# Gated MLP in a two-layer trunk: order of the first products of two pairs, place of the sums of squares and of the scales

## The chip, the cores and the metric

The kernel runs on one core of a Trainium2 chip. The metric is the device time of one execution, in microseconds. Of the kernel before, three executions were timed: 2381.71, 2385.93 and 2390.98, median 2385.93. One more execution was profiled.

## What is computed

Two layers of a decoder trunk over 1040 positions (16 meta tokens and 1024 tokens) of 1024 numbers, in float32. Layer 0 mixes by a short convolution and a gated DeltaNet, layer 1 by attention in a sliding window. Behind each mixer stands the same gated MLP with a causal convolution of width 3 on its gate half. The change is in that MLP alone.

```python
D_MODEL = 1024
SEQ = 1024
N_META = 16
D_FF = 2816
...
def rms_norm(x, w):
    xf = x.astype(jnp.float32)
    y = xf * lax.rsqrt(jnp.mean(xf * xf, -1, keepdims=True) + EPS)
    return (y * w.astype(jnp.float32)).astype(x.dtype)
...
def conv_ffn(h, w_up, conv_w, w_down):
    gate, val = jnp.split(h @ w_up, 2, -1)
    gate = causal_dwconv(gate, conv_w)
    return (jax.nn.silu(gate) * val) @ w_down
...
    for layer in range(DEPTH):
        i = layer // 2
        hn = rms_norm(h, attn_norm_w[layer])
        ...
        h = h + mix.astype(h.dtype)
        ff = conv_ffn(rms_norm(h, ffn_norm_w[layer]), ffn_w_up[layer], ffn_conv_w[layer], ffn_w_down[layer])
        h = h + ff.astype(h.dtype)
    return h[:, N_META:]
```

## The kernel before

The activations lie with the 1024 features on partitions, as eight tiles `h[0..7]` of 128 x 1040. All products are made in float32 precision from two parts: an operand is split into a high part (a cast to the matmul format, on ScalarE, called ACT) and a low part (operand minus high part, on VectorE, called DVE), and TensorE (PE) adds up high x high, high x low and low x high.

`ffn` (L706) makes the up projection in 22 pairs (`NF`). Pair i is one block of 128 gate columns (weights `wg`) and one block of 128 value columns (`wv`). The two token halves and the two feature halves make a 2 x 2 block product that is done with seven products instead of eight, in the manner of Strassen and Winograd. Each of the seven has an operand X0 to X6, built once per layer on ACT and DVE out of `h` and the norm's weights (`parts`, L746; four 128 x 520 pieces with high and low part each, X63 being the last piece of X6), and weights that are `wg`, `wv` or sums of their halves: `sa` (L876, L877) and `sb` (L887, L888). The norm's scale per token, `rstd`, is applied only to the result (L904). A product is 24 matmuls: two token quarters, four feature pieces, three part products.

In each pair X0, X2, X4 and X5 go one after the other into the PSUM tile `A`, with copies `p1`, `u2`, `u3` taken in between on ACT (`snap`, L829). X1 goes into a tile `C`, X3 and X6 into another `C`. `A` and `C` have two buffers each. From these copies come `r` (gate) and `v` (value): `r` takes X1's tile (L871) and X6's (L903), is scaled (L904), convolved and passed through tanh (L851 to L860), and multiplied with `v` (L906); `v` takes X3's tile (L894) and X5's (L898). X6 is added into the same PSUM tile that L894 reads, so X6 waits for L894. The product is stored (`fy`) and read again by the down projection, as `yf`, scaled (L927) and split (L928, L929).

Entry of the MLP: the squares of `h` are summed over the eight tiles into a tile `r` (L737 to L741). `scales` (L758) multiplies the sums with ones on PE (L761) into a `C` tile and finds `rstd` from it on ACT and DVE (L765 to L770), for each token half. The source has both scales ahead of pair 0. The residual stream `h` is stored to memory (`hd`, L735) while its operands are built in place.

Who sets the order: the code is written in program order, and a scheduler of the framework lists each engine's instructions from it, moving them ahead or back by its own estimates; each engine then runs its list strictly in order. `issue_after` holds a part back behind a given instruction. All loads and stores are issued on the SP queue. The matmuls of the out projections ahead of the MLP (L147) use a ring of PSUM tiles `mm` that are freed by the adds into `h` (L699 in layer 0, L1188 in layer 1; two buffers in layer 1). Weights are split into `whi` (L814) and `wlo` (L815), in buffers that turn over three places, one in pool `fp` and two in pool `wp`. The down projection's first weights (`wdr`, cast `wdh` L134 on ACT, low part `wdl` L135 on GpSimd, called POOL) use the buffers of `wp` too.

## Time and profile before

| | |
|---|---|
| median of three executions | 2385.93 us (2381.71 to 2390.98) |
| the profiled execution's own time | 2385.68 us |
| its span in the profile | 2383.9 us |
| mean granted TensorE clock | 0.994 |
| PE busy | 2324.3 us (98%) |
| DVE busy | 1615.8 us (68%) |
| ACT busy | 973.4 us (41%) |
| POOL busy | 408.2 us (17%) |

The MLP of layer 0 starts at 583.78 us of the span and its up projection ends near 1041; that of layer 1 starts at 1668.55 and ends near 2134.

How to read the lines in the prediction. A row of the timeline gives start and length in us, engine, source line, operation, output and input by the program's names, and in brackets how long the engine stood idle before it and what released it. A row of the wait table gives engine, waiting group and releaser, then the total, the number of waits and the longest. A row of the windows gives a stretch, its length, the busy time of PE, PEld (weight loads), DVE, ACT and POOL with the number of instructions, the granted clock, the DMA share and GB/s. A row of the chain gives start, length and the group that lies on the chain of work that ended last. Lengths on DVE include a start-up that overlaps the instruction before, so the distance from start to start is the cost of one.

### The profile page before, as it was taken

How to read it: one execution, taken by the hardware profiler on the slowest of the kernel's cores; microseconds unless marked ns; L12 is line 12 of the kernel's file. 1: busy time of each engine (PE TensorE's matmuls, PEld its weight loads, DVE VectorE, ACT ScalarE, POOL GpSimd, SP SyncE). 2: the span in 40 equal slices, each digit the busy share in tenths (PEclk: the TensorE clock that was granted, in tenths of full speed). 3: DMA queues.
4: the chain of work that ended last, by engine and by line, in shares of the span. 5: the costliest groups of instructions: out<-in, count | busy, mean ns of one | idle time of the engine just before them, and what ended most of it. 6: DMA issues, size and time to landing. Idle time of an engine off the chain costs nothing.

```text
span 2383.9 us, 39785 instructions
## 1 busy us (share of the span) xinstructions
PE 2324.3 (98%) x16000; PEld 2182.5 (92%) x16000; DVE 1615.8 (68%) x2799; ACT 973.4 (41%) x1952; POOL 408.2 (17%) x357
## 2 busy tenths in 40 slices
PE   8999999999999999999999999999899999999999
PEld 7989999999999999999999986778799999987887
DVE  8886745566877777777436466768977777778332
ACT  6544313434444444433116456656544444443110
POOL 1123323431000000012225233231000000002221
PEclk9999999999999999999999999999899999999999
DMA  4233534241222222154223110203222222234222
GB/s 139 79 128 121 170 111 138 76 161 72 89 81 81 81 76 76 63 188 139 66 60 129 45 36 19 89 27 116 81 89 81 81 81 77 72 142 169 76 67 102
DMA packets 93481, 224.83 MB, mean 94 GB/s; under 512 B 18672, under 2 KB 30264, under 8 KB 93296
## 3 DMA queue, kind: packets, MB, share of 16 engines
q1 hardware_dynamic: 93296, 222.28, 27.1%
q8 instruction: 126, 2.06, 0.3%
q14 instruction: 59, 0.48, 0.1%
HBM read 166.08 MB, written 56.15 MB: 93 GB/s over the span
## 4 chain that ended last, share of the span: by engine, by line
PE 84%; DVE 10%; ACT 3%; DMA 1%; issue 1%; POOL 0%; SPq 0%; ACTq 0%; DVEq 0%; POOLq 0%
PE mm L147 40%; PE A L825 20%; PE C L825 15%; PE scp L1067 1%; DVE qt L251 1%; PE po L1122 1%; DVE X L752 1%; PE qkp L971 1%; PE po L1125 1%; ACT xh L182 0%; DVE Xd L499 0%; DVE yl L171 0%; DVE fq L497 0%; DMA rb<-rq 0%; PE ptp L1096 0%
## 5 line engine op out<-in xcount | busy, mean ns | idle before, releaser
L825 PE MATMUL A<-X,whi 128*128 128x260 f32 (+1 forms) x2816 | 513.3, 283 | 5.6 <-ACT whi L814 3.2
L147 PE MATMUL mm<-y,wdh 128*128 128x346 f32 (+2 forms) x1760 | 471.0, 350 | 1.6 <-DVE r L903 1.6
L825 PEld LDWEIGHTS A<-X,whi 128*128 128x128 f32 x2816 | 434.0, 189 | 7.2 <-ACT whi L814 3.6
L825 PE MATMUL C<-X,whi 128*128 128x260 f32 (+1 forms) x2112 | 393.7, 285 | 7.8 <-DVE v L894 5.9
L825 PE MATMUL A<-X,wlo 128*128 128x260 f32 (+1 forms) x1408 | 392.6, 283 | 1.3 <-DVE wlo L815 1.3
L147 PEld LDWEIGHTS mm<-y,wdh 128*128 128x128 f32 x1760 | 315.1, 188 | 32.7 <-DVE r L903 2.0
L135 POOL TENSOR_TENSOR wdl<-wdr,wdh 128x512 fp32r<-128x512 f32 (+1 forms) x80 | 118.8, 1485 | 1311.7 <-ACT wdh L134 1302.4
L825 PEld LDWEIGHTS C<-X,whi 128*128 128x128 f32 x2112 | 330.7, 190 | 8.9 <-DVE v L894 6.3
L147 PE MATMUL mm<-y,wdl 128*128 128x346 f32 (+2 forms) x880 | 307.5, 350 | 0.6 <-POOL wdl L135 0.6
L825 PE MATMUL C<-X,wlo 128*128 128x260 f32 (+1 forms) x1056 | 297.5, 284 | 0.0
L825 PEld LDWEIGHTS A<-X,wlo 128*128 128x128 f32 x1408 | 264.2, 189 | 1.5 <-DVE wlo L815 1.5
L939 DVE TENSOR_TENSOR h<-mm,h 128x346 f32<-128x346 f32 (+2 forms) x200 | 115.9, 584 | 201.8 <-PE mm L147 201.0
L825 PEld LDWEIGHTS C<-X,wlo 128*128 128x128 f32 x1056 | 200.4, 190 | 0.0
L147 PEld LDWEIGHTS mm<-y,wdl 128*128 128x128 f32 x880 | 165.5, 188 | 16.8 <-POOL wdl L135 1.3
L815 DVE TENSOR_TENSOR wlo<-sa,whi 128x1024 fp32r<-128x1024 f32 x44 | 53.9, 1226 | 161.8 <-ACT whi L814 161.8
L134 ACT CAST wdh<-wdr 128x512 fp32r<-128x512 f32 (+1 forms) x80 | 53.1, 663 | 255.6 <-PE mm L147 221.9
L814 ACT CAST whi<-sb 128x512 fp32r<-128x512 f32 x88 | 54.7, 621 | 132.7 <-PE C L825 131.0
L147 PE MATMUL mm<-xl,wqkvh 128*128 128x346 f32 (+1 forms) x288 | 95.8, 333 | 1.4 <-DVE xl L183 1.4
L147 PE MATMUL mm<-xh,wqkvh 128*128 128x346 f32 (+1 forms) x288 | 96.3, 337 | 0.7 <-DVE row L269 0.7
L814 ACT CAST whi<-sa 128x1024 fp32r<-128x1024 f32 x44 | 46.1, 1048 | 115.7 <-PE A L825 115.0
L147 PE MATMUL mm<-xh,wqkvl 128*128 128x346 f32 (+1 forms) x288 | 93.0, 325 | 0.0
L928 ACT CAST y<-yf 128x346 fp32r<-128x346 f32 (+2 forms) x110 | 54.7, 536 | 93.1 <-DVE yf L927 73.7
(391 smaller groups left out, 5054.1 us busy)
## 6 DMA issues: line engine op xcount, KB each, us to landing
wg<-in_w_up SPq DMA_DIRECT2D x44, 512.0 KB, 3.2
wv<-in_w_up SPq DMA_DIRECT2D x44, 512.0 KB, 3.3
wdr<-in_w_down SPq DMA_DIRECT2D x48, 256.0 KB, 2.6
fy<-sg SPq DMA_DIRECT2D x22, 520.0 KB, 2.7
yf<-fy SPq DMA_DIRECT2D x22, 520.0 KB, 4.1
fy<-sg SPq DMA_DIRECT2D x22, 516.0 KB, 2.7
yf<-fy SPq DMA_DIRECT2D x22, 516.0 KB, 4.7
wdr<-in_w_down SPq DMA_DIRECT2D x32, 320.0 KB, 3.5
```

Source lines behind the costliest of these rows:

```text
L134: ac.copy(hi, raw)
L135: eng.tensor_tensor(lo, raw, hi.bitcast(F32), ALU.subtract)
L147: pe.matmul(ps[:, :n], a[:, j, :], b[:, c0:c0 + n], start=(i == 0), stop=(i == last))
L251: ve.scalar_tensor_tensor(d, buf[:, pad + c0 - i:pad + c0 - i + n], taps[W - 1 - i], tmp[:, :n], ALU.mult, ALU.add)
L752: last_lo[:] = [ve.tensor_tensor(lo, src, hi.bitcast(F32), ALU.subtract).ins]
L814: ac.copy(hi, src)
L815: ve.tensor_tensor(lo, src, hi.bitcast(F32), ALU.subtract)
L825: pe.matmul(ps[:, b, :q], a[:, at + k, :], x[:, c], start=(start and n == 0), stop=(n == 11), skip_group_check=not start)
L928: ac.copy(yh[:, s], yf[:, s])
L939: ve.tensor_tensor(hn[m][:, s], ps[:, :n], hn[m][:, s], ALU.add)
L971: pe.matmul(p2[:, :n], ct[:, C_BD:C_BD + P], sq, start=True, stop=True)
L1067: pe.matmul(ps[:, :nk], qg[G][t][r, tok], kx[G][r, cols], start=True, stop=True)
```

## The change

Five things. (1) Pair 0's weights are loaded, and their sums `sa0`, `sb0` and the split of `sa0` are written, ahead of everything else in `ffn`. The pools of raw weights are swapped between odd and even pairs, and the three-place rotation of the split weights is shifted. (2) The squares are summed in the two halves of `rstd` instead of an `r` tile. (3) The two `scales` stand behind pair 0's third product (X2) instead of ahead of pair 0; they work in place in `rstd`, with an `sg` and a `th` tile for scratch. (4) The first two products of pair 1 (X0, X1) are written right behind the first two of pair 0. (5) `v` has two buffers instead of one; the four t2 pieces of the operands lie in two `v` tiles, and the separate t2 tiles are gone. The number of products, sums and casts stays the same.

```diff
+                    nw = [0]
+
+                    def wtile():
+                        nw[0] += 1
+                        p = fp if nw[0] == 1 or nw[0] > 2 and nw[0] % 3 == 2 else wp
+                        t = tuple(p.tile([P, KT, P], F32R, tag=tag, name=tag) for tag in ("whi", "wlo"))
+                        return t
...
+                    def weights(i):
+                        raws = []
+                        for n, at in (("wg", i), ("wv", NF + i)):
+                            r = (wp if i % 2 else fp).tile([P, KT, P], F32, tag="wraw", name=n, **({} if i % 2 else {"bufs": 2}))
+                            sp.dma_start(r, w_up[layer, at])
+                            raws.append(r)
+                        return raws
+
+                    def s21(raws):
+
+                        (wg, wv) = raws
+                        sa = fp.tile([P, KT, P], F32, tag="ws", name="sa", bufs=2)
+                        ve.tensor_tensor(sa[:, 4:8], wv[:, 0:4], wv[:, 4:8], ALU.add)
+                        ve.tensor_tensor(sa[:, 0:4], sa[:, 4:8], wg[:, 0:4], ALU.subtract)
+                        return sa
...
+                    raws0 = weights(0)
+                    sa0 = s21(raws0)
+                    w20 = wtile()
+                    wsplit(w20, 0, KT, sa0)
+                    sb0 = s34(raws0, sa0)
+
+
+                    ss = [rstd[:, tk[s]] for s in range(2)]
-                    sums = full("r", 2)
-                    ss = [sums[:, s * hf:s * hf + hf] for s in range(2)]
...
-                        t = full("th")[:, :hf]
-                        ay = full("sg")
+                        ay, t = full("th" if s else "sg"), rstd[:, tk[s]]
...
-                            ve.scalar_tensor_tensor(rstd[:, tk[s]] if i else y, t, m3, y, ALU.add, ALU.mult)
+                            ve.scalar_tensor_tensor(t if i else y, t, m3, y, ALU.add, ALU.mult)
...
-                    vt2 = full("v")
-                    t2 = [half("t2", 2, "t2") if k < 2 else vt2[:, (k - 2) * hf:(k - 1) * hf] for k in range(4)]
+                    vt2 = [full("v", 2) for _ in range(2)]
+                    t2 = [vt2[k // 2][:, k % 2 * hf:(k % 2 + 1) * hf] for k in range(4)]
...
                     half_x = last_lo[0]
-                    for s in range(2):
-                        scales(s)
...
-                        p = fp if nw[0] % 3 == 0 else wp
...
-                            r = (fp if i % 2 else wp).tile([P, KT, P], F32, tag="wraw", name=n, **({"bufs": 2} if i % 2 else {}))
...
-                        raws = weights(i)
+                        raws = weights(i) if i else raws0
...
+                    def second(w1, p1):
+
                         Bk = wide("C")
                         product(Bk, w1, 4, 1, True)
                         r = full("r", 2)
                         ve.memset(r[:, 0:2], 0.0)
                         ve.tensor_tensor(two(r[:, 2:2 + hf]), Bk[:, :, :q], two(p1), ALU.add)
+                        return r
+
+
+                    nxt = first(0)
+                    rs = [second(*nxt[1::2])]
+                    ahead = first(1)
+                    rs.append(second(*ahead[1::2]))
+                    for i in range(NF):
+                        (wg, wv), w1, A, p1 = nxt
+                        v2 = wv[:, 4:8]
+                        r = rs[i] if i < 2 else second(w1, p1)
+                        if i == 0:
+                            sa, w2, sb = sa0, w20, sb0
+                        else:
+                            with tc.issue_after(half_x) if i == 1 else nullcontext():
+                                sa = s21((wg, wv))
+                                w2 = wtile()
+                                wsplit(w2, 0, KT, sa)
                         product(A, w2, 0, 2, False)
                         u2 = snap("u2", A)
+                        if i == 0:
+                            for s in range(2):
+                                scales(s)
...
-                        v = full("v")
+                        v = full("v", 2)
                         ve.tensor_tensor(two(v[:, hf:2 * hf]), two(u3), C[:, :, :q], ALU.subtract)
                         if i + 1 < NF:
-                            nxt = first(i + 1)
+                            nxt = first(i + 1) if i else ahead
```

What that does to the lists of the engines is shown at three places. Line numbers of the changed kernel differ: L852 is the product's matmul (L825 before), L804 the scale's (L761), L741 the weights' low part (L815), L784 the sum of squares (L741), L755 and L756 `sa`, L763 and L764 `sb`, L923 `v` (L894), L879 and L935 the end of the gate (L860, L906), L958 the split of `y` (L929), L798 an X piece (L755), L1217 the add into `h` (L1188).

First, PE at the start of the MLP of layer 0, before. L147 is the end of the out projection, X03 the last piece of X0, X10 the first of X1. This is where the second scale stands:

```order
L825 MATMUL A_6163<-X03_6031,whi_6159 128x260 x2
L825 MATMUL A_6163<-X03_6031,wlo_6160 128x260
L761 MATMUL C_6098<-r_5969,ct_68 128x260 x2
L825 MATMUL C_6190<-X10_6034,whi_6159 128x260 x2
L825 MATMUL C_6190<-X10_6034,wlo_6160 128x260
L825 MATMUL C_6190<-X11_6037,whi_6159 128x260 x2
```

The first scale stands right behind the out projection, the second between X0 and X1 of pair 0. After the change both scales stand here, on the same engine (A_6145 is pair 0's tile):

```order
L852 MATMUL A_6145<-X23_6082,whi_5976 128x260 x2
L852 MATMUL A_6145<-X23_6082,wlo_5977 128x260
L804 MATMUL C_6289<-rstd_69,ct_68 128x260 x2
L852 MATMUL A_6145<-X40_6098,whi_6338 128x260 x2
L852 MATMUL A_6145<-X40_6098,wlo_6339 128x260
L852 MATMUL A_6145<-X41_6102,whi_6338 128x260
L804 MATMUL C_6301<-rstd_69,ct_68 128x260 x2
```

Ahead of these rows PE now has X0 and X1 of pair 0, X0 and X1 of pair 1, and X2 of pair 0; both scales moved behind those five products, into the start of X4.

Second, DVE in the second to last part of the attention's output projection (layer 1), before. `h6` and `h7` are tiles of the residual stream, `wol` a weight's low part, X a piece of an operand:

```order
L1188 TENSOR_TENSOR h6_16829<-mm_17266,h6_16829 128x334
L135 TENSOR_TENSOR wol_17333<-wor_17330,woh_17332 128x1024
L755 SCALAR_TENSOR_TENSOR X12_17579<-h5_16590,vt_66,X12_17579 128x516
L1188 TENSOR_TENSOR h6_16829<-mm_17280,h6_16829 128x346
L741 TENSOR_TENSOR r_17508<-r_17508,sq_17527 128x516
L1188 TENSOR_TENSOR h7_16874<-mm_17294,h7_16874 128x334
```

The same stretch on DVE after the change:

```order
L755 TENSOR_TENSOR sa_17508<-wv_17506 128x512
L763 TENSOR_TENSOR sb_17515<-wg_17504,wv_17506 128x512
L798 SCALAR_TENSOR_TENSOR X02_17576<-h4_16541,vt_66,X02_17576 128x516
L784 TENSOR_TENSOR rstd_69<-rstd_69,sq_17529 128x516
L135 TENSOR_TENSOR wol_17329<-wor_17326,woh_17328 128x1024
L1217 TENSOR_TENSOR h6_16825<-mm_17262,h6_16825 128x334
L756 TENSOR_TENSOR sa_17508<-sa_17508,wg_17504 128x512
L798 SCALAR_TENSOR_TENSOR X12_17588<-h5_16586,vt_66,X12_17588 128x516
L1217 TENSOR_TENSOR h6_16825<-mm_17276,h6_16825 128x346
L784 TENSOR_TENSOR rstd_69<-rstd_69,sq_17536 128x516
L764 TENSOR_TENSOR sb_17515<-sa_17508,wg_17504 128x512
L741 TENSOR_TENSOR wlo_17512<-sa_17508,whi_17511 128x1024
```

Pair 0's four weight sums and the low part of `sa` stand between the adds into `h`; before, the first of them stood ahead of the last add, and the others behind it.

Third, DVE at the end of the up projection of layer 0 (pair 21), before. `v` here is written from the copy `u3` and X3's tile:

```order
L858 SCALAR_TENSOR_TENSOR sg<-r,hcf,sg 128x1040
L927 TENSOR_TENSOR yf<-yf,rstd 128x348
L927 TENSOR_TENSOR yf<-yf,rstd 128x346 x2
L860 SCALAR_TENSOR_TENSOR sg<-th,sg 128x1040
L929 TENSOR_TENSOR y<-yf,y 128x348
L929 TENSOR_TENSOR y<-yf,y 128x346 x2
L906 TENSOR_TENSOR sg<-sg,v 128x1040
L894 TENSOR_TENSOR v<-u_10971,C 128x520
```

The same place on DVE after the change:

```order
L877 SCALAR_TENSOR_TENSOR sg<-r,hcf,sg 128x1040
L956 TENSOR_TENSOR yf<-yf,rstd 128x348
L956 TENSOR_TENSOR yf<-yf,rstd 128x346 x2
L923 TENSOR_TENSOR v<-u_10967,C 128x520
L879 SCALAR_TENSOR_TENSOR sg<-th,sg 128x1040
L958 TENSOR_TENSOR y<-yf,y 128x348
L958 TENSOR_TENSOR y<-yf,y 128x346 x2
L935 TENSOR_TENSOR sg<-sg,v 128x1040
```

The write of `v` moved ahead of the gate's last step, of the split of `y` and of the reader of the old `v`. On ACT the cast `wdh` of the first down-projection weight stands one step ahead of the copy into `v` that ends X5; before, it stood among the `y` casts ahead of the last copy `u3`.

More of the change, by code (lines that the diff above doesn't have):

```diff
@@ L729, in full, with wsplit, s34 @@
                         return fp.tile([P, 2 + 2 * hf], F32, tag=tag, name=tag, bufs=bufs)
-                    sums = full("r", 2)
-                    ss = [sums[:, s * hf:s * hf + hf] for s in range(2)]
+                    nw = [0]
[4 more added lines that the diff above has]
+                        return t
+                    def wsplit(t, at, n, src):
+                        hi, lo = (x[:, at:at + n, :] for x in t)
+                        ac.copy(hi, src)
+                        ve.tensor_tensor(lo, src, hi.bitcast(F32), ALU.subtract)
+                    def weights(i):
[11 more added lines that the diff above has]
+                        return sa
+                    def s34(raws, sa):
+                        (wg, wv) = raws
+                        sb = fp.tile([P, KT, P], F32, tag="ws", name="sb", bufs=2)
+                        ve.tensor_tensor(sb[:, 0:4], wg[:, 0:4], wv[:, 0:4], ALU.subtract)
+                        ve.tensor_tensor(sb[:, 4:8], sa[:, 0:4], wg[:, 4:8], ALU.subtract)
+                        return sb
+                    raws0 = weights(0)
[4 more added lines that the diff above has]
+                    ss = [rstd[:, tk[s]] for s in range(2)]
                     for j, k in enumerate((0, 4, 1, 5, 2, 6, 3, 7)):
@@ L802, in ffn @@
                             parts(6, k, B(1, k, 1), w[4 + k])
-                    nw = [0]
-                    def wtile():
-                        nw[0] += 1
-                        p = fp if nw[0] % 3 == 0 else wp
-                        t = tuple(p.tile([P, KT, P], F32R, tag=tag, name=tag) for tag in ("whi", "wlo"))
-                        return t
-                    def wsplit(t, at, n, src):
-                        hi, lo = (x[:, at:at + n, :] for x in t)
-                        ac.copy(hi, src)
-                        ve.tensor_tensor(lo, src, hi.bitcast(F32), ALU.subtract)
                     def product(ps, wt, at, j, start):
@@ L832, in snap @@
                         return t
-                    def weights(i):
-                        raws = []
-                        for n, at in (("wg", i), ("wv", NF + i)):
-                            r = (fp if i % 2 else wp).tile([P, KT, P], F32, tag="wraw", name=n, **({"bufs": 2} if i % 2 else {}))
-                            sp.dma_start(r, w_up[layer, at])
-                            raws.append(r)
-                        return raws
                     def first(i):
-                        raws = weights(i)
+                        raws = weights(i) if i else raws0
                         w1 = wtile()
@@ L861, in conv @@
                         return sg
-                    nxt = first(0)
-                    for i in range(NF):
-                        (wg, wv), w1, A, p1 = nxt
-                        g1, g2, v1, v2 = wg[:, 0:4], wg[:, 4:8], wv[:, 0:4], wv[:, 4:8]
+                    def second(w1, p1):
                         Bk = wide("C")
@@ L871, in ffn @@
                         ve.tensor_tensor(two(r[:, 2:2 + hf]), Bk[:, :, :q], two(p1), ALU.add)
[L873 to L878 removed]
+                        return r
[14 more added lines that the diff above has]
+                                wsplit(w2, 0, KT, sa)
                         product(A, w2, 0, 2, False)
                         u2 = snap("u2", A)
+                        if i == 0:
+                            for s in range(2):
+                                scales(s)
                         C = wide("C")
                         product(C, w2, 4, 3, True)
[L884 removed]
                         w3 = wtile()
                         with tc.issue_after(half_x) if i < 2 else nullcontext():
[L887 to L888 removed]
+                            if i:
+                                sb = s34((wg, wv), sa)
                             wsplit(w3, 0, 4, sb[:, 0:4])
```

9 lines of the change are left out of this document (removed).

## The prediction

> **What bounds the kernel now.** I read the page first, then the table of what TensorE waited for, then the windows around both MLP entries and both MLP ends.
>
> ```profile
> span 2383.9 us, 39785 instructions
> PE 2324.3 (98%) x16000; PEld 2182.5 (92%) x16000; DVE 1615.8 (68%) x2799; ACT 973.4 (41%) x1952; POOL 408.2 (17%) x357
> PE 84%; DVE 10%; ACT 3%; DMA 1%; issue 1%; POOL 0%; SPq 0%; ACTq 0%; DVEq 0%; POOLq 0%
> PE C L761 <- DVE r L741: 8.9, 2, 7.9
> PE C L825 <- DVE v L894: 5.9, 2, 3.1
> ```
>
> TensorE is busy 98% of the span, and the chain that ended last lies on it for 84%. So only its idle time and its slow clock can be won. Two of the three largest entries of the wait table (the third is in the first norm) are inside the MLP: 8.9 us for the sums of squares, in two waits, and 5.9 us for `v`, in two waits of up to 3.1 us.
>
> ```profile
> 500.00:520.00 20.00, 19.30 (x122) 19.00 (x121) 10.67 (x18) 5.68 (x8) 4.81 (x2) 1.00 0.85 323
> 560.00:580.00 20.00, 20.00 (x128) 20.00 (x127) 11.66 (x15) 6.41 (x9) 2.57 (x1) 1.00 0.21 80
> 600.00:604.00 4.00, 3.86 (x21) 3.86 (x22) 4.00 (x7) 2.13 (x4) 0.00 (x0) 0.60 0.58 227
> 630.00:650.00 20.00, 20.00 (x169) 20.00 (x168) 16.78 (x23) 8.88 (x12) 0.00 (x0) 1.00 0.25 92
> 1655.00:1665.00 10.00, 9.96 (x63) 9.71 (x62) 9.86 (x16) 5.82 (x9) 0.00 (x0) 1.00 0.75 264
> 1673.00:1680.00 7.00, 0.00 (x0) 0.00 (x0) 7.00 (x12) 5.21 (x10) 0.00 (x0) 0.64 0.12 50
> ```
>
> The columns are stretch, length, busy PE, PEld, DVE, ACT, POOL, granted clock, DMA share, GB/s. In the settled loop (630 to 650) PE has no idle time, and DVE works 16.78 of 20. The entries differ. In layer 0, DVE is half idle ahead of the entry (10.67 and 11.66 of 20) and full behind it (4.00 of 4). In layer 1, DVE is full already during the attention's output projection (9.86 of 10), and PE stands still from 1673 to 1680. So work moved ahead of the entry is nearly free in layer 0 and is paid for in layer 1.
>
> **Entry of layer 0.** First the loss of before.
>
> ```profile
> 583.78 1.04 PE L761 MATMUL C<-r,ct 128*128 128x260 f32 x4
> 588.68 1.15 PE L761 MATMUL C<-r,ct 128*128 128x260 f32 x4 [0.97 <-DVE r L741]
> 598.36 0.39 PE L825 MATMUL A<-X,whi 128*128 128x260 f32 x1 [2.52 <-ACT whi L814]
> 600.14 0.80 PE L825 MATMUL C<-X,whi 128*128 128x260 f32 x2 [1.40 <-DVE r L871]
> 610.71 0.51 PE L825 MATMUL A<-X,whi 128*128 128x260 f32 x2 [0.68 <-ACT u L831]
> 622.59 2.88 PE C L825 x24
> ```
>
> A product is 24 matmuls and takes 2.88 us (last row, of the chain), 0.12 us a matmul. That row ends the 11th product, the fourth of pair 1, at 625.47. Without any wait, 264 matmuls and the two scale groups (0.69 us each, from start to next start) would have ended at 583.78 + 1.38 + 31.7 = 616.9. The loss is 8.6 us: waits of 0.97 + 2.52 + 1.40 + 0.68 = 5.6, some 1.5 for the clock of 0.60 in 600 to 604, and small gaps.
>
> After the change, the order puts four products (X0 and X1 of both pairs) and pair 0's X2 ahead of the first scale. That is 14.4 us of matmuls, and none needs the scale. The four additions of pair 0's weight sums and the low part of `sa` now all lie among the early adds of `h`, from about 510 on, where DVE has room; before, `sb` and that `wlo` came behind the last add. Is DVE fast enough behind it? From its row spacing an addition or subtraction takes 0.605 us, a scalar form 0.67, a 1024-wide `wlo` 1.14:
>
> ```profile
> 1675.40 1.23 DVE L815 TENSOR_TENSOR wlo<-sa,whi 128x1024 fp32r<-128x1024 f32 x1
> 1676.54 0.69 DVE L752 TENSOR_TENSOR X<-v,X 128x516 fp32r<-128x516 f32 x1
> 1686.15 2.75 DVE L797 SCALAR_TENSOR_TENSOR h<-h,vt,h 128x516 f32<-128x516 f32 x4
> 1692.09 0.69 DVE L887 TENSOR_TENSOR sb<-wg,wv 128x512 f32<-128x512 f32 x1
> 1692.69 0.69 DVE L888 TENSOR_TENSOR sb<-sa,wg 128x512 f32<-128x512 f32 x1
> 584.49 0.51 DVE L699 TENSOR_TENSOR h<-mm,h 128x346 f32<-128x346 f32 x1
> ```
>
> Between the last add of `h` (584.49, last row) and the last operand X63, the order now has 27 additions, 14 scalar forms and two `wlo`: 16.3 + 9.4 + 2.3 = 28.0 us, so X63 is there at 612.9. PE has 243 matmuls ahead of it and would ask for it at 583.78 + 1.38 + 29.2 = 614.4. DVE is just in time, and PE sets the pace. I leave 1.2 us for two short waits (A X4 for the copy `u2`, queued on ACT behind `p1` of pair 1, and for X4's low part), each near the 0.68 of the same kind above. Further on, DVE has a backlog when pair 1's later products come: I charge 1.8, between nothing and 0.68 + 1.40 = 2.1, near the upper end since DVE was full until 612. Gain: 8.6 - 1.2 - 1.8 = **5.6**. Bounds: 8.6 if no wait stays; 2.4 if DVE remains the limit, which has lost only the work that moved (2 x 0.605 + 1.14).
>
> **Entry of layer 1.**
>
> ```profile
> 1668.55 1.03 PE L761 MATMUL C<-r,ct 128*128 128x258 f32 x4
> 1680.38 2.09 PE L761 MATMUL C<-r,ct 128*128 128x258 f32 x4 [7.93 <-DVE r L741]
> 1711.13 0.38 PE L825 MATMUL C<-X,whi 128*128 128x258 f32 x1 [0.53 <-DVE X L755]
> 1718.83 3.21 PE A L825 x27
> 1666.51 1.23 DVE L815 TENSOR_TENSOR wlo<-wg,whi 128x1024 fp32r<-128x1024 f32 x1 [0.91 <-ACT whi L814]
> 1671.23 0.51 DVE L1188 TENSOR_TENSOR h<-mm,h 128x346 f32<-128x346 f32 x1
> 1710.32 0.76 DVE L755 SCALAR_TENSOR_TENSOR X<-h,vt,X 128x516 fp32r<-128x516 f32 x1
> ```
>
> Here the wait of 7.93 goes, but DVE pays. Pair 0's four sums and a second `wlo` now stand among the adds of `h`, at which the projection's matmuls wait for their two PSUM buffers; before, one sum and one `wlo` did. That is 3 x 0.605 + 1.14 = 2.96 us more. DVE's only idle time of size there is 0.91 (fifth row), so the last add and PE's first MLP matmul come 2.0 us later: the add is done at 1671.66 + 2.0 = 1673.7, and PE starts at 1670.6.
>
> From that add to X63, before had 38 additions, 20 scalar forms, two `wlo`: 38.7 us, which fits 1671.66 to 1710.98. The order of the change has 33, 18 and two: 20.0 + 12.1 + 2.3 = 34.3. X63 is there at 1708.0, 3.0 us earlier. Before, PE had done 201 of the 264 matmuls when X63 came, and the 63 left took from 1711.13 to 1718.83; now 218 come ahead of it and 46 are left, 5.5 us. The milestone is 1708.0 + 0.2 + 5.5 = 1713.7, or 5.1 better. PE has room for this: its 218 matmuls and scales would be done at 1698.2, so some 10 us of waits (for `u2` behind ACT's casts, for the scale's buffers) are hidden behind DVE. For the backlog that follows I charge 1.5, between nothing and the small waits that this entry has now after 1680 (the 0.53 above; the layer-0 kind 0.68 + 1.40). Gain **3.6**. Bounds: 3.0 + 4.7 = 7.7, if X63 leaves only the last 24 matmuls (63 - 24 = 39, 4.7 us); and -2.0, if the price is paid and X63 comes no earlier.
>
> A clock rule bears on this. Before, a wait of 7.93 us was followed by 0.50 to 0.64 of the clock; the 2.75 below costs as well:
>
> ```profile
> 1680.00:1684.00 4.00, 3.62 (x13) 3.25 (x14) 3.09 (x7) 3.95 (x8) 0.00 (x0) 0.50 0.00 0
> 2129.49 4.40 PE C L825 x24
> ```
>
> The Trainium skill (TensorE: Matmul & The Clock Gate, Part 1: The HAM clock gate) says the clock halves after an idle window of about 3.4 us that runs freely. The trace agrees with the first row and is harsher in the second, where 2.75 us of idle time sufficed. By the rule the changed layer-1 entry, with a wait of some 3.4 us ahead of A X4, would lose about 1.5 us to the clock, and the sum would be 15.0 in place of 16.5.
>
> **The ends of both MLPs.** `v` had one buffer. Its write (L894) therefore stood behind the reader of the old `v` (L906), which stood behind the conv and three subtractions of the down projection's `y`, while PE's last product X6 waited for the PSUM that L894 reads.
>
> ```profile
> 1033.61 1.23 DVE L860 SCALAR_TENSOR_TENSOR sg<-th,sg 128x1040 f32<-128x1040 f32 x1
> 1037.38 0.70 DVE L894 TENSOR_TENSOR v<-u,C 128x520 f32<-128x520 f32 x1
> 1038.13 0.51 PE L825 MATMUL C<-X,whi 128*128 128x260 f32 x2 [3.12 <-DVE v L894]
> 2129.49 0.80 PE L825 MATMUL C<-X,whi 128*128 128x258 f32 x2 [2.75 <-DVE v L894]
> ```
>
> With two buffers the order has `v` where L860 stood: it is done near 1034.3, before PE ends X5 (1038.13 - 3.12 = 1035.0), so the wait of 3.12 goes. In layer 1 likewise, and with it the clock: X6 took 4.40 there, 1.52 over 2.88. Upper bounds: 3.4 (X6 started slowly too) and 4.3.
>
> What is late next is the first down-projection weight. Its cast `wdh` now waits for the end of X5 (it takes the buffer of the weights that X5 reads) and stands behind the `y` casts on ACT; POOL's `wdl` follows:
>
> ```profile
> 1029.04 2.25 POOL L135 TENSOR_TENSOR wdl<-wdr,wdh 128x512 fp32r<-128x512 f32 x1 [464.39 <-ACT wdh L134]
> 1041.97 1.28 POOL L135 TENSOR_TENSOR wdl<-wdr,wdh 128x512 fp32r<-128x512 f32 x1 [10.68 <-ACT wdh L134]
> 1030.06 2.33 DVE L858 SCALAR_TENSOR_TENSOR sg<-r,hcf,sg 128x1040 f32<-128x1040 f32 x1
> ```
>
> Cast near 1035.1 to 1035.7, then 1.28 to 2.25: ready between 1037.1 and 1038.0. X6 ends at 1037.9, and the third matmul behind it needs `wdl`. It is just covered; I charge 0.3 in layer 0 and 0.1 in layer 1. Without that cover it costs us for us, up to all of the gain. The Trainium skill (SBUF — State Buffer, Who interferes with whom) says that a DVE instruction with two SBUF inputs and a POOL instruction that reads SBUF block each other; the first and third rows agree (2.25 and 2.33 beside each other; the same `wdl` alone 1.28). By that rule the moved `wdl` falls beside the `y` subtractions, and the later 1038.0 is the one to take, 0.1 at most against X6's end. Gains: **3.1** and **4.2**; lower bound 0 each.
>
> Edits that cost nothing: squares are added in `rstd` instead of `r`, with as many instructions; the half tiles of t2 lie in `v`; one pair of weights more is loaded ahead of the entry, where the DMA share falls to 0.21 (560 to 580). If the DMA were full there, the sums of that pair would be late by the excess.
>
> **Sum.** 5.6 + 3.6 + 3.1 + 4.2 = 16.5 us. The profiled execution took 2385.68, practically the median of 2385.93 (three runs from 2381.71 to 2390.98). So 2385.9 - 16.5 = 2369.4.
>
> **Rivals.**
> 1. Entries at their lower ends (DVE stays the limit in both): 2.4 - 2.0 + 7.3 = 7.7, **2378.2**. For: DVE's full windows. Against: 34.3 in place of 38.7 us of work. Chance 0.24.
> 2. The down weight takes the place of `v` (late `wdl`, both ends win nothing): 5.6 + 3.6 = 9.2, **2376.7**. For: the cover is 0.1 to 1 us. Against: the times worked out above end with X6. Chance 0.08.
> 3. Slower: the loop's weight buffers rotate in another phase and raw weights sit in the other pool, so one split in each pair may wait until a product has read its buffer, and PE for the split. Price by the one such wait that the trace has:
>
> ```profile
> 1695.17 0.39 PE L825 MATMUL A<-X,wlo 128*128 128x258 f32 x1 [1.30 <-DVE wlo L815]
> ```
>
> 1.30 in 42 settled pairs is 54.6; less 16.5 that is **2424.0**. It makes the kernel slower by over 0.5% from (12 + 16.5) / 42 = 0.68 us a pair. For: every pair uses the new buffers. Against: the order inside a settled pair is the same but for `v`'s reader, and PE had no wait there at all (20.00 of 20). Chance 0.10.
> 4. All upper ends: 8.6 + 7.7 + 3.4 + 4.3 = 24.0, **2361.9**. Chance 0.08.
>
> The forecast keeps 0.50. A measurement of this kernel tells about 0.5%, 12 us, from no change: forecast and rival 4 are faster (0.58), rivals 1 and 2 the same (0.32), rival 3 slower (0.10). Range: from 2359, rival 4's time less 3 us of the scatter, to 2388, the sum of all lower ends (0.4 us won: 2385.5) plus as much; left out is mainly rival 3.
>
> **What would show it.** No PE wait for `v` over 1 us at either end, X6 of layer 1 in 2.9 us; no wait of 8 us behind the attention's output projection, which lasts some 2 us longer; the 11th product some 7 us (layer 0) and 5 us (layer 1) earlier against its out projection's start; PE 20.00 of 20 in the settled loop. Wrong if PE waits in settled pairs, if `wdl` ends later than X6, or if the attention's output projection grows by over 5 us.

## The result and the profile after

The changed kernel takes 2365.39 us (median of five, 2364.93 to 2368.43); the kernel before, with two more executions taken beside it, 2388.03 (2381.71 to 2390.98). The ratio is 0.9913, with a 95% interval of 0.9898 to 0.9928: faster by 0.7 to 1.0%, some 21 us. Forecast were 2369.4 us and a gain of 16.5; the time lies in the stated range, and the gain was larger by about a quarter. The profiled execution took 2365.22 us (before 2385.68).

The page of the changed kernel, with the rows that answer to those of before, and its table of what PE waited for (engine and group, releaser, total, number, longest):

```profile
span 2363.4 us, 39732 instructions
PE 2319.1 (98%) x16000; PEld 2176.2 (92%) x16000; DVE 1605.2 (68%) x2799; ACT 973.5 (41%) x1952; POOL 412.0 (17%) x357
PE 84%; DVE 9%; ACT 3%; DMA 2%; issue 1%; POOL 1%; SPq 0%; ACTq 0%; DVEq 0%; POOLq 0%
```

```profile
PE A L852 <- ACT u L858: 5.3, 5, 3.4
PE mm L147 <- DVE h L1217: 2.8, 3, 1.9
PE mm L147 <- POOL wdl L135: 1.0, 1, 1.0
```

The two large MLP entries of before are gone: nothing is left for the sums of squares (8.9 us) or for `v` (5.9). In their place stand 5.3 us for the copies `u` (2.0 before; 3.4 of it in one wait) and 2.8 us for `h`. The 1.0 for `wdl` falls into the down projection of layer 0 (at 1096.92; 0.32 in the second profile).

The span parts into five stretches: up to the first MLP matmul of layer 0; to its first down matmul; to the first MLP matmul of layer 1; to its first down matmul; to the end. The marks are rows of PE, such as 583.78 and 1668.55 in the prediction and these four of the changed kernel (timeline of PE: start, length, line, tiles):

```profile
579.65 0.40 PE L852 MATMUL A<-X,whi 128*128 128x260 f32 x2
1027.93 0.47 PE L147 MATMUL mm<-y,wdh 128*128 128x348 f32 x2
1658.09 0.40 PE L852 MATMUL A<-X,whi 128*128 128x258 f32 x2
2114.22 0.62 PE L147 MATMUL mm<-y,wdh 128*128 128x512 f32 x2
```

"Before" and "changed" are the first profiles; each was profiled a second time below.

| stretch, us | before | before, 2nd | changed | changed, 2nd | changed less before | forecast |
|---|---|---|---|---|---|---|
| ahead of the MLP of layer 0 | 583.78 | 583.62 | 579.65 | 583.68 | -4.1 | 0 |
| up projection of layer 0 | 458.27 | 460.88 | 448.28 | 448.29 | -10.0 | -8.7 |
| down, attention, its output projection | 626.50 | 624.88 | 630.16 | 629.36 | +3.7 | +2.0 |
| up projection of layer 1 | 466.12 | 465.12 | 456.13 | 455.32 | -10.0 | -9.8 |
| down of layer 1 to the end | 249.2 | 249.8 | 249.2 | 249.2 | 0 | 0 |
| span | 2383.9 | 2384.3 | 2363.4 | 2365.8 | -20.5 | -16.5 |

By the first profiles the three stretches that the forecast priced give -16.3 of its -16.5, and the other 4.1 us lie where both programs list the same instructions. By the second profiles the three give -17.9 (-12.6, +4.5, -9.8) and the span differs by 18.5. Part of the difference is the clock: in the first profile of before a stretch at half clock (0.50 in 1490.6 to 1494.0) falls into the attention, and none does in its second profile or in either of the changed kernel, so that the third row's +3.7 is too small a price.

The entry of layer 0 on PE, all rows with a scale or with a wait over 0.2 us in the first 40 us:

```profile
594.20 1.15 PE L804 MATMUL C<-rstd,ct 128*128 128x260 f32 x4
596.00 0.39 PE L852 MATMUL A<-X,whi 128*128 128x260 f32 x1 [0.25 <-DVE X L795]
596.47 1.04 PE L804 MATMUL C<-rstd,ct 128*128 128x260 f32 x4
614.71 0.51 PE L852 MATMUL A<-X,whi 128*128 128x260 f32 x2 [0.46 <-ACT whi L740]
615.62 0.50 PE L852 MATMUL C<-X,whi 128*128 128x260 f32 x2 [0.40 <-DVE r L932]
```

PE runs from 579.65 to 594.20 through five products, as the order said, and meets only short waits behind them; no half clock follows. Before, waits of 5.6 us stood in this stretch.

In layer 1 the wait of 7.93 us is gone too, but not all of what it cost. First the output projection ahead of it, then the entry (timeline of PE), then two windows (PE, PEld, DVE, ACT, POOL busy, granted clock, DMA share, GB/s):

```profile
1637.26 0.43 PE L147 MATMUL mm<-yh,woh 128*128 128x334 f32 x1 [1.87 <-DVE h L1217]
1641.80 0.39 PE L147 MATMUL mm<-yh,woh 128*128 128x346 f32 x1 [0.53 <-DVE h L1217]
1654.20 0.40 PE L147 MATMUL mm<-yh,woh 128*128 128x346 f32 x1 [0.36 <-DVE h L1217]
1672.90 1.03 PE L804 MATMUL C<-rstd,ct 128*128 128x258 f32 x4
1677.35 0.58 PE L852 MATMUL A<-X,whi 128*128 128x258 f32 x1 [3.42 <-ACT u L858]
1678.47 2.09 PE L804 MATMUL C<-rstd,ct 128*128 128x258 f32 x4 [0.53 <-ACT sg L807]
1681.34 0.80 PE L852 MATMUL C<-X,whi 128*128 128x258 f32 x2 [0.78 <-ACT th L807]
```

```profile
1673.00:1680.00 7.00, 3.05 (x10) 1.93 (x8) 7.00 (x12) 5.45 (x9) 0.00 (x0) 0.76 0.00 0
1680.00:1684.00 4.00, 3.22 (x14) 2.67 (x13) 4.00 (x8) 3.34 (x6) 0.00 (x0) 0.50 0.42 135
```

The three waits for `h` were not there before. They come right behind the moved sums: the first follows `sa` and `sb` on DVE (1633.10 and 1633.69 in its timeline). From the first to the last of its 576 matmuls this projection takes 154.7 us in both profiles (1503.19 to 1657.93 in the first), where both of before have 151.1 to 151.2 (1517.23 to 1668.40 in the first): 3.6 us more. In the entry PE then waits 3.42 us for `u2` and goes on at half clock, while DVE is full (7.00 of 7).

At the ends nothing is left. The chain of layer 0 and of layer 1 (start, length, group), then POOL:

```profile
1022.09 3.14 PE A L852 x24
1025.23 2.87 PE C L852 x24
1028.10 16.99 PE mm L147 x106
...
2111.50 2.88 PE C L852 x24
2114.38 15.84 PE mm L147 x68
```

```profile
1025.94 2.25 POOL L135 TENSOR_TENSOR wdl<-wdr,wdh 128x512 fp32r<-128x512 f32 x1 [465.41 <-DVE y L958]
1028.81 1.28 POOL L135 TENSOR_TENSOR wdl<-wdr,wdh 128x512 fp32r<-128x512 f32 x1 [0.62 <-ACT wdh L134]
```

X6 follows X5 at once, and the down projection follows X6 at once. The late `wdl` took the longer of its two times, 2.25, and ended at 1028.19, just as its matmul came (third of those from 1027.93 on); PE did not wait. It was as close as worked out.

### The profile page after: what moved, and what is told of

Its sections match the earlier page's. It is cut to its first block, busy times and chain, and to the rows that moved or that the text cites. A ratio compares the mean times of both kernels' runs of the same rounds, so it can differ in the third digit from the quotient of the medians.

```text
span 2363.4 us, 39732 instructions
## 1 busy us (share of the span) xinstructions
PE 2319.1 (98%) x16000; PEld 2176.2 (92%) x16000; DVE 1605.2 (68%) x2799; ACT 973.5 (41%) x1952; POOL 412.0 (17%) x357
## 4 chain that ended last, share of the span: by engine, by line
PE 84%; DVE 9%; ACT 3%; DMA 2%; issue 1%; POOL 1%; SPq 0%; ACTq 0%; DVEq 0%; POOLq 0%
PE mm L147 40%; PE A L852 20%; PE C L852 15%; DVE qt L251 1%; PE scp L1096 1%; PE po L1151 1%; DMA fh<-h 1%; DVE fq L497 1%; DVE Xd L499 1%; PE qkp L1000 0%; ACT xh L182 0%; PE po L1154 0%; DVE X L795 0%; PE ptp L1125 0%; DMA rb<-rq 0%
## 5 line engine op out<-in xcount | busy, mean ns | idle before, releaser
L852 PE MATMUL A<-X,whi 128*128 128x260 f32 (+1 forms) x2816 | 512.9, 283 | 6.8 <-ACT u L858 5.3
L147 PE MATMUL mm<-y,wdh 128*128 128x346 f32 (+2 forms) x1760 | 471.7, 351 | 0.0
L852 PEld LDWEIGHTS A<-X,whi 128*128 128x128 f32 x2816 | 433.0, 189 | 9.5 <-ACT u L858 7.3
L852 PE MATMUL A<-X,wlo 128*128 128x260 f32 (+1 forms) x1408 | 392.0, 282 | 0.0
L852 PE MATMUL C<-X,whi 128*128 128x260 f32 (+1 forms) x2112 | 390.3, 283 | 1.2 <-ACT th L807 0.8
L147 PEld LDWEIGHTS mm<-y,wdh 128*128 128x128 f32 x1760 | 315.3, 188 | 31.3
L852 PEld LDWEIGHTS C<-X,whi 128*128 128x128 f32 x2112 | 328.1, 189 | 2.1 <-ACT th L807 1.5
L147 PE MATMUL mm<-y,wdl 128*128 128x346 f32 (+2 forms) x880 | 307.8, 351 | 1.0 <-POOL wdl L135 1.0
L852 PE MATMUL C<-X,wlo 128*128 128x260 f32 (+1 forms) x1056 | 296.4, 283 | 0.0
L852 PEld LDWEIGHTS A<-X,wlo 128*128 128x128 f32 x1408 | 264.3, 189 | 0.0
L852 PEld LDWEIGHTS C<-X,wlo 128*128 128x128 f32 x1056 | 200.0, 190 | 0.0
L147 PEld LDWEIGHTS mm<-y,wdl 128*128 128x128 f32 x880 | 165.5, 188 | 17.1 <-POOL wdl L135 1.3
L741 DVE TENSOR_TENSOR wlo<-sa,whi 128x1024 fp32r<-128x1024 f32 x44 | 53.9, 1226 | 169.5 <-ACT whi L740 169.5
L147 PE MATMUL mm<-xl,wqkvh 128*128 128x346 f32 (+1 forms) x288 | 95.8, 333 | 1.5 <-DVE xl L183 1.5
L147 PE MATMUL mm<-xh,wqkvh 128*128 128x346 f32 (+1 forms) x288 | 96.4, 337 | 0.8 <-DVE row L269 0.7
L147 PE MATMUL mm<-xh,wqkvl 128*128 128x346 f32 (+1 forms) x288 | 93.0, 325 | 0.0
```

Source lines behind the costliest of these rows:

```text
L147: pe.matmul(ps[:, :n], a[:, j, :], b[:, c0:c0 + n], start=(i == 0), stop=(i == last))
L741: ve.tensor_tensor(lo, src, hi.bitcast(F32), ALU.subtract)
L852: pe.matmul(ps[:, b, :q], a[:, at + k, :], x[:, c], start=(start and n == 0), stop=(n == 11), skip_group_check=not start)
```

## The experiments

The first two repeat both kernels, each of the others is one edit; times are medians beside executions of the kernel before on the same chip (medians 2387.2 to 2387.4), with the ratio to it and its 95% interval.

### The kernel before, a second profile

> The kernel before, unchanged, profiled a second time. The first profiles differ by 4.1 us already ahead of the MLP of layer 0 (first MLP matmul at 583.8 before, 579.7 after), where both programs list the same instructions in the same order. Theory A (scatter of single executions: a DMA that lands later, a half-clock window of 3.4 us that falls or does not): this profile starts the MLP anywhere between 578 and 585, and the stretches inside the MLP repeat to within 1 us (entry of layer 0 to its first down matmul 458.3, layer 1 466.1). Theory B (the program before really is slower there): it starts at 583 to 585 again.

2386.68 us, ratio 1.0002 (0.9992 to 1.0012). It starts the MLP at 583.62 again, which by itself spoke for theory B. The up projections gave 460.88 and 465.12: off by 2.6 and 1.0, so that theory A's "within 1 us" failed as well. The reason is in the chain, at the ends of the two up projections:

```profile
1038.14 5.58 PE C L825 x24
...
2130.60 3.13 PE C L825 x24
```

The wait ahead of the first was 3.12 as in the first profile, where X6 then took 3.15; now it took 5.58. The wait ahead of the second was 2.76, and X6 took 3.13, where it had taken 4.40 behind a wait of 2.75. The same wait costs 0 to 2.4 us more, as half clock falls behind it or not.

### The changed kernel, a second profile

> The changed kernel, unchanged, profiled a second time, on the chip on which the next three run. Its first profile reached the MLP of layer 0 at 579.7 where five profiles of other versions did at 583.6 to 584.4. Theory A (that was scatter): it starts at 583 to 585 now, the stretch inside the MLP of layer 0 repeats at 448 and that of layer 1 at 456 us to within 1.5 us, and the time is 2366 to 2371. Theory B (a lasting side effect of the program, for instance of where its buffers in memory lie): 579 to 580 again, 2364 to 2366.

2367.60 us (2366.38 to 2370.06), ratio 0.9921 (0.9909 to 0.9934). The MLP starts at 583.68, the up projections take 448.29 and 455.32: theory A. So the 4.1 us ahead of the MLP were scatter of the first profile and no part of the change. Part of them is a wait in the first mixer (`kq` for `qk`), which was 0.6 to 0.9 us long in three of the twelve profiles, that one among them, and 3.1 to 3.2 in the other nine, of both kernels and of versions of either.

### One buffer for v in the changed kernel

```diff
-                    vt2 = [full("v", 2) for _ in range(2)]
-                    t2 = [vt2[k // 2][:, k % 2 * hf:(k % 2 + 1) * hf] for k in range(4)]
+                    vt2 = full("v")
+                    t2 = [half("t2", 2, "t2") if k < 2 else vt2[:, (k - 2) * hf:(k - 1) * hf] for k in range(4)]
...
-                        v = full("v", 2)
+                        v = full("v")
```

> The changed kernel with one buffer for v, and the two separate t2 tiles back. Theory A (v's second buffer gives what the two ends won): the waits of X6 for v come back at both ends, 2.5 to 3.5 us each, with the wait of the first down matmul for r (0.8 each) and in one of the two a half-clock window (1.5); time 2372 to 2375, 7 to 9 us over the changed kernel, and the entries stay as they are. Theory B (the early order of products is what shortens the ends too, since pair 21 is reached in another phase): no wait for v over 1 us, time within 3 us of 2365.

2373.33 us, ratio 0.9940 (0.9927 to 0.9952), 6 to 8 us over the changed kernel (its second and its first set). PE at both ends (timeline), and the window behind the first (columns as above):

```profile
1031.84 0.50 PE L852 MATMUL C<-X,whi 128*128 128x260 f32 x2 [2.36 <-DVE v L923]
2120.28 0.50 PE L852 MATMUL C<-X,whi 128*128 128x258 f32 x2 [2.26 <-DVE v L923]
```

```profile
1032.00:1037.00 5.00, 5.00 (x29) 5.00 (x30) 0.60 (x1) 0.62 (x1) 0.18 (x2) 0.66 0.74 221
```

Both waits are back (theory A), shorter than before, and one brings half clock (0.66 in 1032 to 1037). The up projection of layer 0 took 452.59 us, 4.3 more than in the changed kernel. That of layer 1 took 455.42, no more than the 456.13 and 455.32 of the changed kernel: its 264th product matmul came 1.1 to 1.9 us earlier, against the expectation that the entries stay as they are, which about makes up for the 2.26. So the time shows theory A, but of the two ends only that of layer 0 shows in its stretch. Before, the first down matmul also waited for `r` at each end:

```profile
1042.05 0.59 PE L147 MATMUL mm<-y,wdh 128*128 128x348 f32 x2 [0.79 <-DVE r L903]
2134.67 0.50 PE L147 MATMUL mm<-y,wdh 128*128 128x512 f32 x1 [0.79 <-DVE r L903]
```

These waits did not come back with the single buffer: X6 is followed at once. That part of the expectation missed.

### The v buffers alone, in the kernel before

The same edit the other way round, in the kernel before.

> The kernel before with only the second buffer for v (t2 in two v tiles). Theory A (parts add up): both ends lose their waits, 7 to 9 us faster than the kernel before, about 2378; the entries keep the 8.9 us of waits for the sums. Theory B (the buffer only helps together with the new order): less than 4 us.

2378.04 us, ratio 0.9953 (0.9939 to 0.9966), 8 to 15 us won. The end of layer 0 in its chain:

```profile
1033.53 3.13 PE A L825 x24
1036.66 2.89 PE C L825 x24
1039.55 0.02 issue
1039.58 0.71 DVE r L903
1040.33 3.77 PE mm L147 x22
```

X6 follows X5 at once, so the buffer by itself removes the wait for `v`; the wait for `r` (0.79) stays. The latter therefore belongs to another part of the change, and not to the buffer. Neither of the two moves of products brings it back by itself: with pair 1 in its old place, or with the scales back in front (both below), the first down matmul waits for nothing either. The entries are as before (9.5 us for the sums). Theory A: the buffer alone brings about 9 us of the 20. In this profile the up projections are 2.1 to 4.7 us (layer 0) and 3.7 to 4.7 us (layer 1) shorter than in the two of before.

### Pair 1 in its old place

```diff
-                    ahead = first(1)
-                    rs.append(second(*ahead[1::2]))
...
-                        r = rs[i] if i < 2 else second(w1, p1)
+                        r = rs[i] if i < 1 else second(w1, p1)
...
-                            nxt = first(i + 1) if i else ahead
+                            nxt = first(i + 1)
```

> The changed kernel without the move of pair 1: its first two products stand where the kernel before has them; scales, sums and v buffers as changed. Theory A (those 48 matmuls, 5.8 us, are what PE works on while DVE builds X2 to X4): in layer 0 the entry grows by 2 to 5 us (the 264th product matmul comes 36 to 39 us after the start, not 34.3), in layer 1 by 1 to 4 us; time 3 to 8 us over the changed kernel. Theory B (the moved scales and sums do it all, and the scheduler brings the products of pair 1 ahead by itself): within 2 us of it.

2372.34 us, ratio 0.9940 (0.9928 to 0.9952), 5 us over the second run of the changed kernel. The 264th product matmul starts 37.7 us after the MLP's first product matmul in layer 0 (34.3 in both profiles of the changed kernel) and 47.5 in layer 1 (43.3 and 42.5). The up projections grow by 1.7 us in layer 0 and by 3.0 to 3.8 in layer 1, so that half of the 3.4 us in layer 0 is made good behind this mark. Theory A: these 48 matmuls are what PE works on while DVE builds the operands.

### The scales back in front

```diff
                     half_x = last_lo[0]
+                    for s in range(2):
+                        scales(s)
...
-                        if i == 0:
-                            for s in range(2):
-                                scales(s)
```

> The changed kernel with both scales back ahead of the products; pair 1's products ahead, sums and v buffers as changed. Theory A (the wait for the sums of squares is the largest loss of the entries, and only the place of the scales removes it): in layer 1 PE waits for the sums between the first product or two and the rest, 4 to 8 us, with half clock behind it; layer 1's entry grows by 3 to 7 us, layer 0's by 0 to 2; time 3 to 8 us over the changed kernel. Theory B (DVE sets the pace of layer 1's entry, so PE's wait only changes its place): layer 1 within 1.5 us of the changed kernel.

2373.58 us, ratio 0.9948 (0.9934 to 0.9961), 6 us over the second run of the changed kernel. In its profile PE waits 2.9 us for the sums in layer 1, not 4 to 8, and the up projections grow by 1.8 (layer 0) and 0.8 to 1.6 us (layer 1), not by 3 to 7 in layer 1. Theory A had the time right, but only a part of it in the place that it named. The profiled execution, 2370.19, was the fastest of its five, so that the two stretches show 3 us of the 6; the rest is not located.

### Layer 1's sums in their old place

```diff
-                    sa0 = s21(raws0)
                     w20 = wtile()
-                    wsplit(w20, 0, KT, sa0)
-                    sb0 = s34(raws0, sa0)
+                    if layer == 0:
+                        sa0 = s21(raws0)
+                        wsplit(w20, 0, KT, sa0)
+                        sb0 = s34(raws0, sa0)
...
-                            sa, w2, sb = sa0, w20, sb0
+                            w2 = w20
+                            if layer == 0:
+                                sa, sb = sa0, sb0
+                            else:
+                                sa = s21(raws0)
+                                wsplit(w2, 0, KT, sa)
...
-                            if i:
+                            if i or layer:
                                 sb = s34((wg, wv), sa)
```

> The changed kernel, where the sums of pair 0's weights and their low part stay early in layer 0 only; in layer 1 they stand in the loop as in the kernel before. Theory A (the 2.8 us of new waits for h in the attention's output projection are the price of those sums, and DVE, which is full there, must do them anyway): the waits for h go, the stretch from the first down matmul of layer 0 to the MLP of layer 1 shrinks by 3 to 3.7 us to about 626.7, and the MLP of layer 1 grows by 2 to 4 us, since the same 3.6 us of DVE work come back ahead of its later products; time within 2 us of the changed kernel. Theory B (moving them early was a loss in layer 1): the MLP of layer 1 does not grow, 3 us faster.

2367.07 us, ratio 0.9919 (0.9905 to 0.9932): the same as the changed kernel. But the edit moved less than was meant. DVE in layer 1 (rows of its timeline; the third is the last add of `h`; the second sum of `sa` stands at 1638.10, that of `sb` at 1678.65):

```profile
1634.67 0.69 DVE L755 TENSOR_TENSOR sa<-wv 128x512 f32<-128x512 f32 x1
1640.39 1.23 DVE L741 TENSOR_TENSOR wlo<-sa,whi 128x1024 fp32r<-128x1024 f32 x1
1660.24 0.51 DVE L1223 TENSOR_TENSOR h<-mm,h 128x346 f32<-128x346 f32 x1
1678.05 0.69 DVE L763 TENSOR_TENSOR sb<-wg,wv 128x512 f32<-128x512 f32 x1
```

The scheduler still set both sums of `sa` and their low part among the adds; only the two sums of `sb`, 2 x 0.605 = 1.2 us, went behind them. The output projection's matmuls took 153.6 us from first to last: 2.4 over before, where the three instructions that stayed come to 2.35, and 1.1 under the changed kernel. The waits for `h` fell from 2.8 to 1.7, and the up projection of layer 1 grew by 1.8 to 2.6, to 457.9. For `sb` that is theory A: it costs about as much on either side of the entry. For the other 2.35 us the experiment doesn't tell.

### The scales behind X3

```diff
-                        if i == 0:
-                            for s in range(2):
-                                scales(s)
                         C = wide("C")
                         product(C, w2, 4, 3, True)
+                        if i == 0:
+                            for s in range(2):
+                                scales(s)
```

> The changed kernel with the scales written behind pair 0's X3 instead of ahead of it. In the changed kernel PE waits 3.42 us in layer 1 for the copy u2, which ACT has queued behind a copy and four casts, and 10.2 us at half clock begin there. Theory A (PE lacks work just there; X3's 24 matmuls, 2.9 us, need only X3 and the weights that are already there): the wait shrinks to under 1 us, the half clock with it; layer 1 wins 3 to 7 us, layer 0 within 1 us; time 2358 to 2363. Theory B (DVE sets the pace, so a wait that goes comes back later at X5 or X6): within 2 us of the changed kernel.

2367.23 us, ratio 0.9915 (0.9901 to 0.9928): no gain, theory B. PE in the entry of layer 1:

```profile
1680.90 0.39 PE L852 MATMUL A<-X,whi 128*128 128x258 f32 x1 [1.00 <-ACT u L858]
1684.84 2.09 PE L804 MATMUL C<-rstd,ct 128*128 128x258 f32 x4 [3.55 <-DVE r L888]
```

The wait for `u2` shrank from 3.42 to 1.00, and a new one of 3.55 came: the scale needs a `C` buffer that DVE empties (L888), and DVE is late. The up projection of layer 1 was 1.2 to 2.0 us shorter in this profile, which the times don't show.

### Layer 1's sums on POOL

```diff
+                    eng0 = gp if layer else ve
-                    sa0 = s21(raws0)
+                    sa0 = s21(raws0, eng0)
                     w20 = wtile()
-                    wsplit(w20, 0, KT, sa0)
-                    sb0 = s34(raws0, sa0)
+                    wsplit(w20, 0, KT, sa0, eng0)
+                    sb0 = s34(raws0, sa0, eng0)
```

> The changed kernel, where pair 0's four weight sums and the low part of sa are made by POOL in layer 1 instead of DVE (layer 0 as changed). POOL has nothing else to do in the attention's output projection. Theory A (the price there is DVE's 3.6 us): the waits for h (2.8 us) go, DVE is 3.6 us ahead at X63, and the stretches from the first down matmul of layer 0 to that of layer 1 shrink by 4 to 6 us together; time 2361 to 2364. Theory B (POOL and DVE hold each other up, as where a wdl on POOL took 2.25 us in place of 1.28 and the DVE instruction beside it 2.33 in place of 1.28): five POOL instructions cost DVE about as much as it saves, within 2 us of the changed kernel (2367).

2373.62 us, ratio 0.9939 (0.9925 to 0.9953): 6 us slower than the second run of the changed kernel, worse than either theory. POOL, DVE and PE in the attention's output projection:

```profile
1636.62 1.29 POOL L755 TENSOR_TENSOR sa<-wv 128x512 f32<-128x512 f32 x1 [6.40 <-DMA wv<-in_w_up]
1637.86 1.57 POOL L763 TENSOR_TENSOR sb<-wg,wv 128x512 f32<-128x512 f32 x1
1639.39 1.53 POOL L756 TENSOR_TENSOR sa<-sa,wg 128x512 f32<-128x512 f32 x1
1641.00 1.42 POOL L764 TENSOR_TENSOR sb<-sa,wg 128x512 f32<-128x512 f32 x1
1636.79 6.01 DVE L171 TENSOR_TENSOR yl<-q,yh 128x346 fp32r<-128x346 f32 x4
1643.28 0.42 PE L147 MATMUL mm<-yh,woh 128*128 128x346 f32 x1 [4.06 <-DVE h L1218]
```

Four DVE subtractions that take 1.80 together in the changed kernel (its row at 1630.95) took 6.01 beside four POOL instructions of 1.3 to 1.6, and PE waited 4.06 for the add behind them. The output projection's matmuls took 159.8 us from first to last, 5.1 more than in the changed kernel, and the up projection of layer 1, 455.9, was no shorter. The Trainium skill (SBUF — State Buffer, Who interferes with whom) has this rule, two SBUF inputs on DVE against a POOL instruction that reads SBUF; here each of the four subtractions took 1.5 to 1.6, as long as the POOL instruction beside it, and DVE lost 4.2 us for the 2.4 us of additions taken over.

### Half of layer 1's squares on POOL

```diff
-                                ve.tensor_tensor(ss[s], ss[s], sq, ALU.add)
+                                (gp if layer and s else ve).tensor_tensor(ss[s], ss[s], sq, ALU.add)
```

> The changed kernel, where in layer 1 the seven additions of squares of the second token half are made by POOL instead of DVE: 4.2 us of DVE work go, 7 to 15 us of POOL work come, in a stretch where POOL is idle. The scale that needs these sums stands behind the fifth product, 14 us after the end of the output projection. Theory A (DVE sets the pace of layer 1's entry): X63 comes 3 to 4 us earlier and the MLP of layer 1 shrinks by 2 to 4 us, time 2363 to 2365. Theory B (the two engines hold each other up): DVE's rows beside POOL's grow by as much as is saved, within 2 us of the changed kernel or slower by up to 3.

2369.94 us (2365.26 to 2371.18), ratio 0.9922 (0.9910 to 0.9935): the same as the changed kernel. Its waits for `h` rose to 4.2 us, the up projection of layer 1 took 454.9, 0.4 to 1.3 less, and the output projection's matmuls took 1.8 more. Theory B in its result; no version tried was measurably faster than the changed kernel.

## Why the prediction was right, and where it was off

**Entry of layer 0 (5.6).** Right in cause and nearly in size. The up projection won 10.0 us by the first profiles; of these the end takes 3.12 (wait) + 0.27 (slow start of X6) + 0.79 (`r`) = 4.2, which leaves 5.8. By the second profiles it is 12.6 less 3.12 + 2.70 + 0.79 = 6.6, which leaves 6.0. X63 was ready at 608.14 + 0.67 = 608.8, 29.2 us after the MLP's start, where 612.9 - 583.78 = 29.1 was worked out. The 264th product matmul came 34.3 us after the start in both profiles, as was worked out without the 1.8 for the backlog. The waits on the way, 0.25, 0.46 and 0.40, come to 1.1 where 1.2 was charged. What the entry had won at that mark, 7.1 to 7.3 us, shrank by 1.3 behind it, where 1.8 was charged. What the early sums bring in layer 0 by themselves was not tested.

**Output projection ahead of layer 1 (+2.0).** The mechanism was right, the size too low: its matmuls took 3.6 us longer, in both profiles. The step that failed is the count "one sum and one `wlo`" for before, less an idle time of 0.91. PE's matmuls use two PSUM buffers in turn, so the last add that PE still waited for is the third to last, and in before it is the first of these rows of DVE:

```profile
1665.09 0.51 DVE L1188 TENSOR_TENSOR h<-mm,h 128x346 f32<-128x346 f32 x1
1669.96 0.69 DVE L876 TENSOR_TENSOR sa<-wv 128x512 f32<-128x512 f32 x1
```

The sum, the `wlo` at 1666.51 and the idle time ahead of it all stand behind that add; PE had sent its last output matmul at 1668.40. So all of the 4 x 0.605 + 1.14 = 3.56 counts, and 3.6 was measured; with `sb` moved back 2.35 counts, and 2.4 was measured. For `sb` this price was not a loss: it came back behind the entry.

**Entry of layer 1 (net 3.6).** The statement that DVE sets the pace there held: removing most of PE's wait for `u2` brought a wait for DVE. X63 was ready 38.4 us after the first MLP matmul (row of 1695.78 and 0.67 less 1658.09) where 37.4 was worked out, and the 264th matmul started at 43.3 and 42.5 us where the milestone, 1713.7 - 1670.6, is 43.1. The prediction's reading of before is a little off here: 206 matmuls, not 201, had started before 1711.13, and the 264th ended near 1718.2, not 1718.83. Of the 10.0 us that the up projection won by the first profiles, the end has 2.75 + 1.52 + 0.79 = 5.1 and the entry 4.9 (5.6 forecast); by the second, 9.8 less 2.76 + 0.25 + 0.79 = 3.8 leaves 6.0. Less the price ahead, 3.6, the net is 1.3 to 2.4 in place of 3.6.

**The ends (3.1 and 4.2).** Right in cause: the buffer alone in the kernel before removes both waits and wins about 9 us, and without it in the changed kernel both waits return, though layer 1's does not lengthen its up projection there. The ends won 4.2 to 6.6 and 3.8 to 5.1. The forecast lacked 0.79 at each end, the first down matmul's wait for `r`; which part of the change removes it is open, as none of the experiments on the changed kernel brought it back. The cover for `wdl` held, with 2.25 us on POOL as the longer case said. The 1.5 us for the clock in layer 1 were not a property of that end: the second profile of before had its half clock in layer 0 instead.

**The sum.** That the priced stretches gave -16.3 where -16.5 was forecast is in part luck: the ends and the entry of layer 0 brought more than forecast, the entry of layer 1 net of its price less, and the half clock in the attention of before hides some of that price.

**The rivals.** "Entries at their lower ends" is refuted in layer 0; in layer 1 the net of 1.3 to 2.4 lies between its -2.0 and the 3.6 of the forecast. "The down weight takes `v`'s place" and "a wait in each settled pair" did not happen: no such row in the wait table. "All upper ends", 2361.9, is nearer to the first five executions than the forecast, but for a reason that it didn't name: the excess over 16.5 us in the first profiles, 4.0, is scatter ahead of the MLP. The second set, 2367.60, is nearer to the forecast.

**The clock rule** (the Trainium skill, TensorE: Matmul & The Clock Gate, Part 1: The HAM clock gate) would, by the prediction's estimate, have had a wait of 3.4 us cost about 1.5. The clock of 0.50 in 1680 to 1684 and 0.76 ahead of it agree that half clock comes with the 3.42 us. What it cost no run separates: in the second profile 6.8 us at half clock come behind a wait of 3.0, in place of 10.2, and the up projection is 0.8 us shorter.

## What to carry to other kernels

Count an engine's work only up to the last thing that the bound engine still waits for: what stands behind that point costs it nothing there, and moved ahead of that point it costs its full length. A buffer count of one can show up at the end of a loop alone, as it did here, and can be tested by itself. The scheduler's list decides what an experiment tests: an edit of the source may move less than it says. Where the pace is set by DVE, taking a wait away from PE moves it, and giving DVE's work to POOL can cost more than it saves.

## What was not expected of the hardware

Half clock may or may not follow a short wait at one and the same place. Waits of 3.12 and 2.75 us, each at one place of one program, were followed by half clock in one execution and not in another (X6 behind 3.12: 3.15, then 5.58; behind 2.75: 4.40, then 3.13). A wait that is removed so takes away its own length and a risk of some 1.5 to 2.4 us. Executions of the kernel before spread over 9 us in the first five, those of the changed kernel over 3.5 and 3.7 in two sets, but that these waits make the spread is not shown: with both waits back (one buffer for `v`) five executions spread over 3.9, and with both gone from the kernel before over 6.0.
